# Nine places instead of seven in the ring of expert rows, the dot product written over its own input, and a 64 KB weight piece for the log gates

## The chip, the cores and the metric

The kernel runs on one core of a Trainium2 chip. The metric is the device time of one execution in microseconds (us). Below, PE is the matmul engine (PEld its weight load), DVE the vector engine, ACT the scalar engine, POOL the engine whose queue also issues the gathers, and SP the queue that issues the plain transfers.

## The reference

Two layers (`DEPTH = 2`) over 256 tokens of 1024 channels in float32. Each layer has a mixer and then an expert retrieval:

```
mix = _mixer(h, ...)                       # projections, gated linear attention, gMLP gating, output projection
h   = _layer_norm(ALPHA * h + mix, ...)
q   = (x @ wq)                             # 8 heads x 2 halves
v1, i1 = top_k(s1, 16); v2, i2 = top_k(s2, 16)
sc, pos = top_k(v1 + v2 of all pairs, 16)  # 16 experts per head: 128 per token
act = gelu(einsum('td,tkd->tk', x, u_tab[eidx]))
out = einsum('tk,tkd->td', softmax(sc) * act, v_tab[eidx])
h   = _layer_norm(ALPHA * h + out, ...)
```

Inside the mixer the log gates come from a narrow projection of 16 columns (`a @ w_gate_up + b_gate`, with `a` of rank 16).

## The kernel before, in words

The 256 tokens are two halves of 128 (one token per partition), so with two layers there are four blocks of retrieval, numbered 0 to 3: (layer 0, half 0), (0, 1), (1, 0), (1, 1). Each block has 128 steps, one for each of the 128 experts of a token, 512 steps in all. The tables `peer_u` and `peer_v` lie side by side in HBM, so a step fetches for each of the 128 tokens one row of 2048 floats, 8 KB.

One step `i` is made of these operations:

- `gather` (L726, POOL's queue): an indirect DMA of 128 rows of 8 KB into a tile `uv` of a ring of `UVBUFS = 7` places. It is issued `AHEAD - 1 = 4` steps early.
- `dot` (L733, DVE): multiplies the first 1024 columns of `uv` by the token's `h` and sums them into one column of `dots`. The elementwise product goes to a scratch tile `junk`.
- `weigh` (L739 to L742, ACT): gelu of the dot, times the softmax weight `ex`, spread on a diagonal matrix `dg` (three places).
- the product (L791, PE): `dg` times the last 1024 columns of `uv`, accumulated over the block in two PSUM banks `bank_acc`. Each product is recorded as four matmuls of 128x512. When it has run, the place in the ring is free.

Beside the 128 steps of a block runs the work of another block, as a generator `side(n, done)`: it finishes the block before (`residual_block`), computes the mixer of the next block (`front`) and its 128 expert numbers per token (`ask`, with the top-16 searches on DVE in `top16` and `retrieve`). After each step as many pieces of this generator are recorded as an allowance `PACE` lets through. A piece's cost is given by its `yield`. Side work of block 3 is only the output of block 2. PE, DVE and ACT execute in the order in which the code records the instructions (`manual_schedule`), while the framework places what POOL and SP do.

Layer norms need one instruction on POOL each, a power (`rrs`, `bnrs` or `ri`, at L161 and L215). It stands in the same queue as the gathers.

The mixer's and the query's weights come as pieces of 128x1024 floats, 512 KB, 45 for each of four passes (`feed_of`, `Feed`), through a ring `raw` of four. ACT rounds each piece to a high part `whi` (L142) and DVE forms the rest `wlo` (L147). The first piece of a pass is `C_A`, the 16 columns of the log gates, padded with zeros to 128 columns. The loop as it stands before:

```
if i > 1:
    m = i - 2
    ... nc.tensor.matmul(acc[hf], lhsT=dgs[m], rhs=uvs[m][...])
if i < N:
    dot(i // K % NB, i % K, uvs[i], chosen[i // K][2])
if 0 < i <= N:
    dgs[i - 1] = weigh((i - 1) % K, *chosen[(i - 1) // K][1:])
if i == 0 or (i > 2 and i % K == 1 and i < N):
    work, debt = side(i // K, acc), 0.0
```

Of the kernel before, what the change touches and what calls it, by code (L numbers as in the profile page):

```python
# [19 lines left out]
L = 2  # L20
T = 256
D = 1024
# [14 lines left out]
UVBUFS, AHEAD = 7, 5  # L37
# [8 lines left out]
C_Q, C_K, C_A, C_SV, C_V, C_R, C_SU, C_OUT, C_WQ = 0, 2, 4, 5, 9, 13, 17, 21, 29  # L46
NCH = 45


class Feed:  # L50
# [9 lines left out]
    def load(self):  # L60
        if self.srcs:
            self.raws.append(self.t.load(self.srcs.pop(0)))
# [37 lines left out]
class Trunk:  # L100
# [34 lines left out]
    def load(self, src):  # L135
        raw = self.raw()
        self.nc.sync.dma_start(raw, src)
        return raw

    def split_hi(self, raw):  # L140
        hi = self.ring.tile([128, 1024], F32R, name="whi", tag="whi", bufs=HI)
        self.nc.scalar.copy(hi, raw)  # L142
        return hi

    def split_lo(self, raw, hi):
        lo = self.ring.tile([128, 1024], F32R, name="wlo", tag="wlo", bufs=LO)
        self.nc.vector.tensor_tensor(lo, raw, hi.bitcast(F32), op=OP.subtract)  # L147
        return lo
# [45 lines left out]
    def wide(self, b, hi, lo, p=None):  # L194


        p = self.bank("a")[:, :256] if p is None else p
        v = p.rearrange("p (e t) -> p e t", e=2)
        for dc in range(DC):
            self.mm(v, [(hi[:, dc * 128:(dc + 1) * 128], self.x[:, b, dc])], dc == 0, False)  # L200
        for dc in range(DC):
            self.mm(v[:, 0], [(lo[:, dc * 128:(dc + 1) * 128], self.xh[:, b, dc])], False, dc == DC - 1)
        return v[:, 0], v[:, 1]
# [367 lines left out]
    def run(self):  # L571
        nc, a, sm = self.nc, self.a, self.sm
        with self.tc.tile_pool(name="peer", bufs=1) as pp:
# [193 lines left out]
            with self.tc.manual_schedule(engines=ORDERED):  # L767
# [13 lines left out]
                for i in range(N + 2):  # L781
# [4 lines left out]
                    if i > 1:  # L786
                        m = i - 2
                        if m % K == 0:
                            acc = [self.bank("acc") for _ in range(2)]
                        for hf in range(2):  # L790
                            nc.tensor.matmul(acc[hf], lhsT=dgs[m], rhs=uvs[m][:, D + hf * 512:D + (hf + 1) * 512],  # L791
                                             start=m % K == 0, stop=m % K == K - 1)
                        del dgs[m], uvs[m]
                    if i < N:
                        dot(i // K % NB, i % K, uvs[i], chosen[i // K][2])
                    if 0 < i <= N:
                        dgs[i - 1] = weigh((i - 1) % K, *chosen[(i - 1) // K][1:])
                    if i == 0 or (i > 2 and i % K == 1 and i < N):
                        for _ in work or []:
                            pass  # L800
                        work, debt = side(i // K, acc), 0.0
                    if work:
                        debt += PACE[min(i // K, 3)]
                        while debt > 0:
# [3 lines left out]
                            debt -= c or 1.5  # L808
                for _ in self.output_block(acc, 1, V_LN2 + V_LAYER):
# [30 lines left out]
def pack(inputs):  # L840
# [17 lines left out]
    wm[:, C_A].reshape(L, 128, DC, 128)[:, :, :, :16] = aw.reshape(L, DC, 128, 16).transpose(0, 2, 1, 3)  # L858
# [8 lines left out]
    for l in range(L):  # L867
# [5 lines left out]
        "vecs": vecs,  # L873
        "wmix": wm, "uv": uv,
# [23 lines left out]
```

## Time and profile before

| | |
|---|---|
| median of 3 runs | 1699.54 us (1698.48 to 1712.32) |
| profiled execution, its own time | 1692.46 us |
| span of the profiled execution | 1690.7 us |
| mean granted PE clock | 0.944 |
| bytes read from HBM | 634.38 MB |
| PE / DVE / ACT / POOL busy | 85% / 71% / 47% / 36% of the span |

The profiled execution is one of several, 1.8 us longer than its span and 7.1 us shorter than the median of the timed runs. The first 139 us have no gather; the last gather is issued at 1662 us. All times of the trace count from the start of the span. In a table of stretches, PEclk is the granted share of the full PE clock, and GB/s is what all DMA engines moved in the stretch.

### The profile page before, as it was taken

To read this page: it belongs to the slowest core of one execution; us is meant where nothing else is said; L and a number is where in the kernel's file an instruction comes from. 1 tells how busy PE (TensorE), PEld (TensorE's weight loads), DVE (VectorE), ACT (ScalarE), POOL (GpSimd) and SP (SyncE) were. 2 spreads that over 40 slices of the span, in tenths; PEclk is the share of its full clock that TensorE was granted. 3 is DMA by queue.
4 is the path that set the end of the run, shared out by engine and by line. 5 is a ranking of instruction groups with operands and counts; after the bars stand their busy time and mean duration, and the time that the engine had idled before them with its cause. 6 is when DMAs were issued, how large, how long until landed. Compare 5 with 4: busy or idle time off the path is not lost.

```text
span 1690.7 us, 17829 instructions
## 1 busy us (share of the span) xinstructions
PE 1430.4 (85%) x4544; PEld 749.1 (44%) x4544; DVE 1204.0 (71%) x2898; ACT 794.7 (47%) x2106; POOL 614.1 (36%) x542
## 2 busy tenths in 40 slices
PE   7887699989878889989887798989977887777776
PEld 5675255646533455445543354545543332222222
DVE  6778977767998667666898566766899654444444
ACT  5643465654544565544444374544444433333332
POOL 0002343444324343444334343444324433333331
PEclk9976999999899999999999898999989989999999
DMA  7647999999989999999989999999989999999996
GB/s 234 224 143 300 347 390 396 416 417 419 404 330 364 392 418 391 419 419 419 396 353 386 402 399 363 418 419 419 419 320 361 409 372 421 422 421 422 421 421 255
DMA packets 102409, 636.60 MB, mean 377 GB/s; under 512 B 11634, under 2 KB 12436, under 8 KB 36772
## 3 DMA queue, kind: packets, MB, share of 16 engines
q0 software_dynamic: 73872, 537.49, 78.3%
q1 hardware_dynamic: 28436, 97.98, 15.3%
q8 instruction: 37, 0.61, 0.1%
q14 instruction: 64, 0.52, 0.1%
HBM read 634.38 MB, written 1.05 MB: 376 GB/s over the span
## 4 chain that ended last, share of the span: by engine, by line
DVE 28%; DMA 24%; issue 19%; PE 14%; POOL 12%; ACT 2%; POOLq 1%; DVEq 0%; SPq 0%; ACTq 0%
DMA uv<-uv,eid 23%; POOL uv L726 11%; DVE junk L733 10%; PE bank_acc L791 7%; PE bank_a L153 5%; DVE wlo L147 3%; DVE i L605 2%; DVE v L603 2%; PE bank_b L179 1%; DVE S L608 1%; DVE sums L650 1%; POOLq L726 1%; DVE pos L605 1%; DVE sums L651 1%; ACT whi L142 1%
## 5 line engine op out<-in xcount | busy, mean ns | idle before, releaser
L791 PE MATMUL bank_acc<-uv,dg 128*128 128x512 f32 x2048 | 1012.3, 629 | 199.0 <-ACT dg L742 187.7
L726 POOL DMA_INDIRECT uv<-uv,eid x512 | 595.8, 1164 | 917.8 <-PE bank_acc L791 599.1
L733 DVE SCALAR_TENSOR_TENSOR junk<-uv,h 128x1024 f32<-128x1024 f32 x512 | 626.8, 1224 | 369.6 <-DMA uv<-uv,eid 364.6
L791 PEld LDWEIGHTS bank_acc<-uv,dg 128*128 128x128 f32 x2048 | 375.6, 196 | 723.4 <-ACT dg L742 383.9
L739 ACT ACTIVATE dots<-dots 128x1 f32<-128x1 f32 x512 | 103.3, 202 | 561.1 <-DVE junk L733 556.6
L147 DVE TENSOR_TENSOR wlo<-raw,whi 128x1024 fp32r<-128x1024 f32 x180 | 218.9, 1219 | 35.0 <-issue 16.9
L742 ACT ACTIVATE dg<-ident,dots 128x128 f32<-128x128 f32 x512 | 205.6, 402 | 38.5 <-PE bank_acc L791 21.9
L142 ACT CAST whi<-raw 128x1024 fp32r<-128x1024 f32 x180 | 187.4, 1044 | 42.9 <-DMA raw<-wmix 23.6
L740 ACT ACTIVATE dots<-dots,ex 128x1 f32<-128x1 f32 x512 | 150.8, 295 | 16.6
L153 PE MATMUL bank_a<-whi,x 128*128 128x512 f32 x384 | 137.2, 465 | 6.4 <-ACT f_sr L520 4.8
L153 PE MATMUL bank_a<-x,whi 128*128 128x256 f32 x672 | 118.9, 325 | 9.3 <-ACT f_half L694 6.1
L153 PEld LDWEIGHTS bank_a<-x,whi 128*128 128x128 f32 x672 | 98.2, 213 | 24.6 <-issue 9.8
L153 PEld LDWEIGHTS bank_a<-whi,x 128*128 128x128 f32 x384 | 72.7, 192 | 48.0 <-issue 27.4
L153 PE MATMUL bank_a<-x,wlo 128*128 128x128 f32 x672 | 91.1, 282 | 0.0
L153 PEld LDWEIGHTS bank_a<-x,wlo 128*128 128x128 f32 x672 | 89.5, 206 | 0.0
L179 PE MATMUL bank_b<-vecs,ident 16*128 16x512 f32 x96 | 58.9, 752 | 23.8 <-DVE f_at L408 11.9
L694 ACT COPY f_half<-bank_a 128x128 f32<-128x128 f32 x64 | 17.0, 265 | 113.6 <-DVE qp L697 109.1
L153 PE MATMUL bank_a<-wlo,x 128*128 128x512 f32 x192 | 66.6, 401 | 2.0 <-DVE wlo L147 1.9
L700 PEld LDWEIGHTS bank_b<-kt,qp 128*128 128x128 f32 x128 | 26.0, 214 | 40.6 <-issue 17.1
L179 PEld LDWEIGHTS bank_b<-vecs,ident 16*128 16x128 f32 x96 | 19.5, 219 | 55.2 <-issue 30.2
L153 PEld LDWEIGHTS bank_a<-wlo,x 128*128 128x128 f32 x192 | 36.3, 191 | 13.3 <-DVE wlo L147 5.2
L733 DVE DVE_READ_ACCUMULATOR junk<-uv,h 128x1 f32 x512 | 42.1, 82 | 0.0
(137 smaller groups left out, 761.6 us busy)
## 6 DMA issues: line engine op xcount, KB each, us to landing
raw<-wmix SPq DMA_DIRECT2D x180, 512.0 KB
uv<-uv,eid POOLq DMA_INDIRECT x512
h<-x SPq DMA_DIRECT2D x2, 512.0 KB
out<-h SPq DMA_DIRECT2D x4, 256.0 KB
f_cM<-gm POOLq DMA_DIRECT2D x1, 576.0 KB
f_sw<-sgwT SPq DMA_DIRECT2D x2, 256.0 KB
f_msk<-gmask SPq DMA_DIRECT2D x1, 320.0 KB
kt<-kT SPq DMA_DIRECT2D x2, 128.0 KB
```

Source lines behind the costliest of these rows:

```text
L142: self.nc.scalar.copy(hi, raw)
L147: self.nc.vector.tensor_tensor(lo, raw, hi.bitcast(F32), op=OP.subtract)
L153: self.nc.tensor.matmul(out, lhsT=l, rhs=r, start=start and i == 0, stop=stop and i == n - 1)
L179: self.nc.tensor.matmul(p, lhsT=self.ident[0:16, row:row + 1].to_broadcast([16, 128]), rhs=self.vecs[:, hf * 512:(hf + 1) * 512], start=Tr ...
L603: nc.vector.max(v[:, r], vals)
L605: nc.vector.max_index(i[:, r], v[:, r], vals)
L726: nc.gpsimd.indirect_dma_start(out=uv, out_offset=None, in_=a["uv"], in_offset=bass.IndirectOffsetOnAxis(ap=eid[:, k:k + 1], axis=0), boun ...
L733: nc.vector.scalar_tensor_tensor(junk, uv[:, :D], 1.0, self.h[:, b], op0=OP.mult, op1=OP.mult, accum_out=dots[:, k:k + 1])
L739: nc.scalar.activation(c, c, AF.Gelu)
L740: nc.scalar.mul(c, c, ex[:, k:k + 1])
L742: nc.scalar.mul(dg, self.ident, c)
L791: nc.tensor.matmul(acc[hf], lhsT=dgs[m], rhs=uvs[m][:, D + hf * 512:D + (hf + 1) * 512], start=m % K == 0, stop=m % K == K - 1)
```

## The change

`UVBUFS, AHEAD` become 9 and 8. The dot writes its elementwise product over the `u` half of its own place instead of `junk`. The product of step `m` is recorded at the end of step `m + 1`, after that step's side work, instead of at the head of step `m + 2`. The side work of a block starts at step 1, 129, 257, 385 (before: 0, 129, 257, 385). The `C_A` piece becomes an array of its own of 128x128 floats, 64 KB, and its matmuls write 16 rows instead of 128.

```diff
-UVBUFS, AHEAD = 7, 5
+UVBUFS, AHEAD = 9, 8
...
-C_Q, C_K, C_A, C_SV, C_V, C_R, C_SU, C_OUT, C_WQ = 0, 2, 4, 5, 9, 13, 17, 21, 29
-NCH = 45
+C_Q, C_K, C_SV, C_V, C_R, C_SU, C_OUT, C_WQ = 0, 2, 4, 8, 12, 16, 20, 28
+NCH = 44
+C_A = -1
...
-            self.raws.append(self.t.load(self.srcs.pop(0)))
+            src = self.srcs.pop(0)
+            raw = self.t.raw()[:, :src.shape[-1]]
+            self.t.nc.sync.dma_start(raw, src)
+            self.raws.append(raw)
...
+        m = hi.shape[-1] // DC
+        v = p[0:m].rearrange("p (e t) -> p e t", e=2)
         for dc in range(DC):
-            self.mm(v, [(hi[:, dc * 128:(dc + 1) * 128], self.x[:, b, dc])], dc == 0, False)
+            self.mm(v, [(hi[:, dc * m:(dc + 1) * m], self.x[:, b, dc])], dc == 0, False)
...
-                junk = pp.tile([128, D], F32, name="junk", tag="junk")
-                nc.vector.scalar_tensor_tensor(junk, uv[:, :D], 1.0, self.h[:, b], op0=OP.mult, op1=OP.mult,
+                u = uv[:, :D]
+                nc.vector.scalar_tensor_tensor(u, u, 1.0, self.h[:, b], op0=OP.mult, op1=OP.mult,
...
-                    if i > 1:
-                        m = i - 2
-                        if m % K == 0:
-                            acc = [self.bank("acc") for _ in range(2)]
-                        for hf in range(2):
...
-                    if 0 < i <= N:
+                    if i > 0:
                         dgs[i - 1] = weigh((i - 1) % K, *chosen[(i - 1) // K][1:])
-                    if i == 0 or (i > 2 and i % K == 1 and i < N):
+                    if i > 0 and (i - 1) % K == 0:
...
-                        work, debt = side(i // K, acc), 0.0
+                        work, debt = side((i - 1) // K, acc), 0.0
+                        acc = [self.bank("acc") for _ in range(2)]
...
+                    if i > 0:
+                        m = i - 1
+                        for hf in range(2):
+                            nc.tensor.matmul(acc[hf], lhsT=dgs[m], rhs=uvs[m][:, D + hf * 512:D + (hf + 1) * 512],
...
-        order += [C_WQ + k for k in range(16)]
-        return Feed(self, [self.a["wmix"][l, c] for c in order])
+        return Feed(self, [self.a["wa"][l] if c == C_A else self.a["wmix"][l, c] for c in order])
```

POOL's queue at the first gathers, before, with the semaphores that each instruction waits for (`DMASW0` to `DMASW7` tell of landings of POOL's DMAs, `PE` and `DVE` of those engines):

```order
L726 DMA uv<-uv,eid 128x2048 [waits DVE_49]
L726 DMA uv<-uv,eid 128x2048 x6
L726 DMA uv<-uv,eid 128x2048 [waits DMASW0_49,DMASW1_49,DVE_49,PE_49]
L726 DMA uv<-uv,eid 128x2048 [waits DMASW2_49,DVE_49,PE_49]
L726 DMA uv<-uv,eid 128x2048 [waits DMASW3_49,DVE_49,PE_49]
```

The same place after the change:

```order
L728 DMA uv<-uv,eid 128x2048 [waits DVE_49]
L728 DMA uv<-uv,eid 128x2048 x6
L728 DMA uv<-uv,eid 128x2048 [waits DMASW0_49]
L728 DMA uv<-uv,eid 128x2048 [waits DMASW1_49]
L728 DMA uv<-uv,eid 128x2048 [waits DMASW2_49,DVE_49,PE_49]
L728 DMA uv<-uv,eid 128x2048 [waits DMASW3_49,DVE_49,PE_49]
```

Nine gathers instead of seven stand ahead of the first that waits for PE. The landings are told by eight semaphores in turn, so from the ninth gather on each also waits for the landing of the one eight before it.

POOL's queue from the first gather of block 0 to the first powers, before:

```order
L726 DMA uv<-uv,eid 128x2048 x28
L215 TENSOR_TENSOR rrs<-rve,mhalf 128x1
L726 DMA uv<-uv,eid 128x2048 x17
L161 TENSOR_TENSOR bnrs<-rs,mhalf 128x1
L726 DMA uv<-uv,eid 128x2048 x21
```

And after:

```order
L728 DMA uv<-uv,eid 128x2048 x32
L217 TENSOR_TENSOR rrs<-rve,mhalf 128x1
L728 DMA uv<-uv,eid 128x2048 x17
L162 TENSOR_TENSOR bnrs<-rs,mhalf 128x1
L728 DMA uv<-uv,eid 128x2048 x21
```

Each power of block 0 stands behind four more gathers than before. In blocks 1 to 3 it is three more (at the first power of block 1: behind 138 gathers instead of 135).

PE in block 0, before, from a query of `ask` to the second row of products (L153 projects, L700 multiplies by the keys):

```order
L153 MATMUL bank_a<-x,whi 128x256 x8
L153 MATMUL bank_a<-x,wlo 128x128 x8
L700 MATMUL bank_b<-kt,qp 128x128
L153 MATMUL bank_a<-x,whi 128x256 x8
L153 MATMUL bank_a<-x,wlo 128x128 x8
L791 MATMUL bank_acc<-uv,dg 128x512 x4
L700 MATMUL bank_b<-kt,qp 128x128
```

And after:

```order
L154 MATMUL bank_a<-x,whi 128x256 x8
L154 MATMUL bank_a<-x,wlo 128x128 x8
L807 MATMUL bank_acc<-uv,dg 128x512 x2
L702 MATMUL bank_b<-kt,qp 128x128
L154 MATMUL bank_a<-x,whi 128x256 x8
L154 MATMUL bank_a<-x,wlo 128x128 x8
L807 MATMUL bank_acc<-uv,dg 128x512 x4
L702 MATMUL bank_b<-kt,qp 128x128
```

In block 0 the side work stands one product later (the program counts two matmuls to a product). From block 1 on, PE, DVE and ACT have the same order as before, side work and steps alike.

## Rows read from the trace of the kernel before

**Rows 1.** The page: engines, the gathers' queue, and the costliest groups.

```profile
PE 1430.4 (85%) x4544; PEld 749.1 (44%) x4544; DVE 1204.0 (71%) x2898; ACT 794.7 (47%) x2106; POOL 614.1 (36%) x542
...
q0 software_dynamic: 73872, 537.49, 78.3%
...
L791 PE MATMUL bank_acc<-uv,dg 128*128 128x512 f32 x2048 | 1012.3, 629 | 199.0 <-ACT dg L742 187.7
L726 POOL DMA_INDIRECT uv<-uv,eid x512 | 595.8, 1164 | 917.8 <-PE bank_acc L791 599.1
L733 DVE SCALAR_TENSOR_TENSOR junk<-uv,h 128x1024 f32<-128x1024 f32 x512 | 626.8, 1224 | 369.6 <-DMA uv<-uv,eid 364.6
```

**Rows 2.** Busy time by stretch: length; PE, PEld, DVE, ACT, POOL; PEclk, DMA share, GB/s.

```profile
139.00:240.00 101.00, 77.59 (x229) 39.74 (x228) 89.77 (x304) 45.72 (x122) 41.07 (x35) 0.86 0.95 365
240.00:440.00 200.00, 189.22 (x705) 112.26 (x704) 147.62 (x289) 113.72 (x281) 80.46 (x66) 0.97 1.01 413
440.00:540.00 100.00, 76.46 (x240) 38.66 (x239) 93.48 (x338) 45.37 (x126) 35.34 (x31) 0.91 0.91 352
540.00:580.00 40.00, 33.09 (x79) 13.80 (x78) 24.98 (x43) 16.66 (x48) 14.59 (x15) 0.91 0.98 395
580.00:820.00 240.00, 220.99 (x783) 124.84 (x783) 167.56 (x315) 130.51 (x334) 103.52 (x81) 0.97 1.01 413
820.00:920.00 100.00, 77.43 (x244) 39.98 (x244) 95.19 (x343) 45.14 (x126) 34.66 (x31) 0.91 0.94 369
920.00:980.00 60.00, 50.18 (x127) 21.80 (x126) 37.36 (x72) 25.12 (x75) 24.06 (x22) 0.91 0.96 391
980.00:1220.00 240.00, 219.76 (x774) 124.16 (x773) 165.68 (x316) 128.40 (x329) 98.56 (x80) 0.96 1.00 409
1220.00:1330.00 110.00, 84.93 (x264) 42.96 (x263) 102.74 (x358) 49.64 (x141) 42.03 (x37) 0.94 0.91 354
1330.00:1380.00 50.00, 43.16 (x79) 15.72 (x78) 26.80 (x47) 15.84 (x54) 19.57 (x19) 0.86 0.94 380
1380.00:1660.00 280.00, 222.70 (x450) 75.94 (x448) 138.14 (x224) 100.57 (x336) 111.78 (x114) 1.00 1.01 421
```

**Rows 3.** POOL's timeline at the end of block 0: start, length, in brackets the idle time before.

```profile
514.27 0.99 POOL L726 DMA_INDIRECT uv<-uv,eid  x1 [2.43 <-DVE S L608]
520.41 1.08 POOL L726 DMA_INDIRECT uv<-uv,eid  x1 [5.16 <-PE bank_acc L791]
...
555.37 0.99 POOL L726 DMA_INDIRECT uv<-uv,eid  x1 [1.49 <-PE bank_acc L791]
557.86 0.99 POOL L726 DMA_INDIRECT uv<-uv,eid  x1 [1.50 <-PE bank_acc L791]
```

**Rows 4.** POOL's timeline where block 2 passes into block 3.

```profile
1353.49 0.99 POOL L726 DMA_INDIRECT uv<-uv,eid  x1 [1.50 <-PE bank_acc L791]
...
1360.20 1.04 POOL L726 DMA_INDIRECT uv<-uv,eid  x1 [0.24 <-issue]
1370.16 1.33 POOL L726 DMA_INDIRECT uv<-uv,eid  x1 [8.93 <-PE bank_acc L791]
```

**Rows 5.** PE's timeline just behind that place.

```profile
1370.53 11.98 PE L791 MATMUL bank_acc<-uv,dg 128*128 128x512 f32 x27
```

**Rows 6.** The page: splitting the weight pieces, and their loads.

```profile
L147 DVE TENSOR_TENSOR wlo<-raw,whi 128x1024 fp32r<-128x1024 f32 x180 | 218.9, 1219 | 35.0 <-issue 16.9
...
raw<-wmix SPq DMA_DIRECT2D x180, 512.0 KB
```

**Rows 7.** POOL's timeline where block 1 passes into block 2.

```profile
961.23 0.56 POOL L215 TENSOR_TENSOR rrs<-rve,mhalf 128x1 f32<-128x1 f32 x1 [5.84 <-DVE rve L548]
962.21 1.04 POOL L726 DMA_INDIRECT uv<-uv,eid  x1 [0.42 <-PE bank_acc L791]
```

**Rows 8.** DVE's timeline at the same place.

```profile
965.68 1.40 DVE L232 SCALAR_TENSOR_TENSOR h<-h,rrs,bank_b 128x512 f32<-128x512 f32 x2
```

**Rows 9.** The gather's line alone by stretch: length, POOL busy, PEclk, DMA share, GB/s.

```profile
440.00:540.00 100.00, 35.34 (x31) 0.91 0.91 352
...
1400.00:1640.00 240.00, 94.91 (x97) 1.00 1.01 421
```

More of the change, by code (lines that the diff above doesn't have):

```diff
@@ L133, in raw @@
         return r
[L135 to L138, printed above, removed]
     def split_hi(self, raw):
         hi = self.ring.tile([128, 1024], F32R, name="whi", tag="whi", bufs=HI)
+        hi = hi[:, :raw.shape[-1]]
         self.nc.scalar.copy(hi, raw)
@@ L146, in split_lo @@
         lo = self.ring.tile([128, 1024], F32R, name="wlo", tag="wlo", bufs=LO)
+        lo = lo[:, :raw.shape[-1]]
         self.nc.vector.tensor_tensor(lo, raw, hi.bitcast(F32), op=OP.subtract)
@@ L197, in wide @@
         p = self.bank("a")[:, :256] if p is None else p
-        v = p.rearrange("p (e t) -> p e t", e=2)
+        m = hi.shape[-1] // DC
+        v = p[0:m].rearrange("p (e t) -> p e t", e=2)
         for dc in range(DC):
-            self.mm(v, [(hi[:, dc * 128:(dc + 1) * 128], self.x[:, b, dc])], dc == 0, False)
+            self.mm(v, [(hi[:, dc * m:(dc + 1) * m], self.x[:, b, dc])], dc == 0, False)
         for dc in range(DC):
-            self.mm(v[:, 0], [(lo[:, dc * 128:(dc + 1) * 128], self.xh[:, b, dc])], False, dc == DC - 1)
+            self.mm(v[:, 0], [(lo[:, dc * m:(dc + 1) * m], self.xh[:, b, dc])], False, dc == DC - 1)
         return v[:, 0], v[:, 1]
@@ L780, in run @@
                 work, debt, acc = None, 0.0, None
-                for i in range(N + 2):
+                for i in range(N + 1):
                     for j in range(0 if i == 0 else i + AHEAD - 1, min(i + AHEAD, N)):
@@ L785, in run @@
                         uvs[j] = gather(chosen[j // K][0], j % K)
-                    if i > 1:
-                        m = i - 2
-                        if m % K == 0:
-                            acc = [self.bank("acc") for _ in range(2)]
-                        for hf in range(2):
-                            nc.tensor.matmul(acc[hf], lhsT=dgs[m], rhs=uvs[m][:, D + hf * 512:D + (hf + 1) * 512],
-                                             start=m % K == 0, stop=m % K == K - 1)
-                        del dgs[m], uvs[m]
                     if i < N:
                         dot(i // K % NB, i % K, uvs[i], chosen[i // K][2])
-                    if 0 < i <= N:
+                    if i > 0:
                         dgs[i - 1] = weigh((i - 1) % K, *chosen[(i - 1) // K][1:])
-                    if i == 0 or (i > 2 and i % K == 1 and i < N):
+                    if i > 0 and (i - 1) % K == 0:
                         for _ in work or []:
                             pass
-                        work, debt = side(i // K, acc), 0.0
+                        work, debt = side((i - 1) // K, acc), 0.0
+                        acc = [self.bank("acc") for _ in range(2)]
                     if work:
-                        debt += PACE[min(i // K, 3)]
+                        debt += PACE[min((i - 1) // K, 3)]
                         while debt > 0:
@@ L808, in run @@
                             debt -= c or 1.5
+                    if i > 0:
+                        m = i - 1
+                        for hf in range(2):
+                            nc.tensor.matmul(acc[hf], lhsT=dgs[m], rhs=uvs[m][:, D + hf * 512:D + (hf + 1) * 512],
+                                             start=m % K == 0, stop=m % K == K - 1)
+                        del dgs[m], uvs[m]
                 for _ in self.output_block(acc, 1, V_LN2 + V_LAYER):
@@ L857, in pack @@
     wm[:, C_K:C_K + 2] = feat(k)
-    wm[:, C_A].reshape(L, 128, DC, 128)[:, :, :, :16] = aw.reshape(L, DC, 128, 16).transpose(0, 2, 1, 3)
     wm[:, C_SV:C_SV + 4] = tok(sv)
@@ L873, in pack @@
         "vecs": vecs,
+        "wa": cc(aw.reshape(L, DC, 128, 16).transpose(0, 2, 1, 3).reshape(L, 128, DC * 16)),
         "wmix": wm, "uv": uv,
```

## The prediction, made blind

> **What bounds the kernel now.** I read the page first: which engine is full, and who waits for whom [rows 1]. No engine is: PE is busy 85% of the span, DVE 71%. The two long waits point at each other. DVE stands 364.6 us in front of its dots until a gather has landed, and POOL stands 599.1 us in front of its gathers until a product on PE has freed a place. So the ring of `uv` turns in a circle of gather, dot, product and free place, and the question is in which stretches the DMA engines are the slow part of it, and in which the ring holds them up.
>
> The table by stretch answers that [rows 2]. In the last, where block 3 has no side work, the DMA engines move 421 GB/s and all else waits: gathers are issued 2.49 us apart (555.37 and 557.86 us, [rows 3]), the time that 1.05 MB (537.49 MB over 512, [rows 1]) takes at that rate. I take 421 as the full rate. Every other stretch falls short of it. Length times (1 - rate/421) is the time in which the DMA engines might have moved bytes and did not:
>
> - four stretches in which DVE is full: 139 to 240 (13.4 us lost), 440 to 540 (16.4), 820 to 920 (12.4), 1220 to 1330 (17.5). DVE is busy 89 to 95% there, with the top-16 searches between the dots.
> - three passages between blocks: 540 to 580 (2.5), 920 to 980 (4.3), 1330 to 1380 (4.9).
> - the middles: 240 to 440 (3.8), 580 to 820 (4.6), 980 to 1220 (6.8). PE is busy 92 to 95% there, and the rate is 409 to 413.
> - 1380 to 1660: nothing.
>
> That is 86.6 us in all, the most that feeding the DMA engines better could bring. How a loss looks is seen in two places. At the end of block 0, POOL issues a gather at 514.27 us and the next at 520.41 [rows 3]: all places hold landed rows, and the DMA engines stand until DVE and ACT have made the next `dg`. Between blocks 2 and 3, gathers go out at 1353.49, 1360.20 and then 1370.16 [rows 4], because PE is held up by the layer norm of the output. What is in flight runs dry before the last of them.
>
> **The ring.** Two more places let two more gathers go out before POOL has to wait. Two gathers are 2 x 2.49 = 5.0 us of DMA time. In a stretch where the ring fills, the DMA engines stop 5.0 us later, and when DVE comes free two more landed rows wait for it. The lead is kept only if the consumers can then go faster than the gathers. They can: behind the halt at 1370 PE runs 27 recorded matmuls, four to a product, in 11.98 us [rows 5], 1.77 us a product against 2.49 for a gather, and a dot takes 1.22 us [rows 1]. Each passage of the ring from empty to full and back thus gains the smaller of its loss and 5.0 us:
>
> - the four stretches with full DVE each lose more than 5.0: 4 x 5.0 = 19.9 us (exactly 4.98 each). The rest of their loss stays, since DVE has that much work.
> - the three passages lose less than 5.0 each, and close: 2.5 + 4.3 + 4.9 = 11.7 us.
> - the middles lose 15.2 us in many short waits. Each is covered by two places, but what PE may still give there is small: it is idle 10.8, 19.0 and 20.2 us, and part of that comes from the order of work, not from missing rows. Bounds 0 and 15.2; I take a third, 5.1 us, nearer to the lower end because of PE's 92 to 95%.
>
> **The product's new place.** From block 1 on nothing moves on PE, DVE and ACT: the product at the end of step m+1 and at the head of step m+2 has the same neighbours, and only POOL's gathers pass the side work's powers. In block 0 the side work comes one product and one dot later. DVE is full there from 139 to 240 and does the same work in another order: 0, with 1.3 us (a dot and its readout) either way.
>
> **Powers behind more gathers.** A power now stands behind three gathers more (four in block 0), the last of which waits for a product one step younger than before. At the passage into block 2 the power ran at 961.23, and the gather behind it followed the product that ended just before 962.21 [rows 7]. After the change that product, with a gather of 1.0 us, comes ahead of the power, so `rrs` is ready at about 963.9 instead of 961.8. Its reader on DVE starts at 965.68 [rows 8], so 1.8 us of cover remain. I price it at 0 and, at the thirteen powers, at up to 1 us each without cover, 13 us for the range.
>
> **The dot in its own place.** DVE's time goes by elements: the split `wlo`, two tensors into a third, takes 1219 ns, the dot 1224 [rows 1, 6]. Writing over an operand instead of `junk` changes neither count. I take 0. The row does not show a write into an operand, so I keep 0.1 us either way for each of the about 125 dots in the four full stretches, 12 us, for the range.
>
> **The small piece.** It saves 448 KB, 0.459 MB, in each of four passes [rows 6]. At 421 GB/s that is 1.09 us. Three of the passes are loaded beside gathers, in a kernel that would now be nearer to DMA's limit: 3.3 us. The first is loaded ahead of all gathers, where the DMA engines are not the limit: 0 to 1.1, I take 0. Its split gets some 1 us shorter on ACT and on DVE at each of the four places; at the passages this lies beside the residual that PE waits for, and the ring now covers that wait. I take 0, and up to 2 us.
>
> **Sum.** 19.9 + 11.7 + 5.1 + 3.3 = 40.0 us. The profiled execution took 1692.5 us, so it would take 1652.5. The median of the timed runs is 7.1 us above the profiled execution, which makes 1659.5 us, the forecast.
>
> **Rivals.**
>
> PE takes over. If PE's idle time in the middles is all structure, the leads won at 139 to 240 (5.0) and at the first two passages (6.8) find no spare PE time behind them and are lost, and the middles give nothing (5.1). That leaves 40.0 - 16.9 = 23.1 us: 1676.4. For it: windows in which PE is busy 92 to 95% [rows 2]. Against: these windows hold waits of DVE for rows too, which get shorter with the lead.
>
> POOL cannot issue. The gathers' issue could be what is short while DVE is full, not the places. Then the four stretches gain nothing, 40.0 - 19.9 = 20.1 us: 1679.4. In such a stretch 31 issues take 35.34 us, 1.14 each, against 0.98 (94.91 over 97) where DVE is half idle [rows 9]. That is 5 us of 100, and POOL stands idle most of the rest. The Trainium skill speaks for this rival (SBUF — State Buffer, "Summary: rules for kernel authors"): descriptors that GpSimd writes are starved while VectorE is in its faster modes. By that rule a deeper ring would be of no use exactly where DVE is full; the trace agrees with a longer issue, by 0.16 us, but not with starving.
>
> One place instead of two. The landings are counted by eight semaphores in turn, and the program's order shows a gather waiting for the landing of the one eight before it. If that binds, the ring acts as eight places: half of the 19.9 and about 2 us of the passages are lost, 28 us remain: 1671.5. Against it: a place is freed by a product, which needs the landing plus dot, weigh and product; so the landing of the younger neighbour, 2.49 us later, is mostly there already.
>
> The places are not the limit at all. Then the small piece alone counts, 3.3 us: 1696.2.
>
> Slower. The powers lock the circle: a power waits behind a gather, the gather for a product, the product on PE behind matmuls of side work that wait for the power before. If each of the thirteen cost two products and a gather on the path, 2 x 2.49 + 1.3 = 6.3 us, that is 82 us against 40: 1741. It decides from 40.0/13 = 3.1 us each. Against it are the 1.8 us of cover shown above, and that a place nine back was freed by a product from before the side work in question.
>
> **How the numbers follow.** Forecast 0.60 (gains of 30 to 50 us: 1650 to 1670). PE takes over 0.18, POOL 0.04, one place 0.06, no limit 0.05, slower 0.03, and 0.04 for more than 55 us, where the middles close wholly and PE's clock (0.86 to 0.97 in the stretches with waits) comes back. The range reaches from 1643, the sum with the middles' upper bound, the first piece and the shorter splits (53 us, with a few us for the spread of runs), to 1682, which takes in PE, POOL and one place and leaves out no limit, slower and some of the edges. A measurement of this kernel tells about 1%, 17 us, from no change. Faster by that much: 0.60 + 0.15 + 0.03 + 0.06 + 0.04 = 0.88. Within it: 0.09, mostly the no-limit case and the tails of PE and POOL. Slower: 0.03.
>
> **What the profile of the changed kernel would show.** The table by stretch: the four stretches with full DVE keep a dip, but each shorter by some 5 us of lost DMA time; the passages show 415 or more. The total wait of POOL for products falls by less than the wait of DVE for rows does, if PE becomes the limit in the middles. The dot's mean stays at 1.22 us and the gather's issue at about 1.0 to 1.2. POOL's first wait for a product comes behind nine gathers. The powers start 0 to 2.5 us later against their inputs, and their readers do not move. The bytes fall by 1.8 MB. The prediction is wrong if the middles come to run below 409 GB/s (PE, not DMA, sets them), if the full stretches lose as much as before (the issue or a semaphore limits), or if DVE waits for `rrs` at the passages.

## The result and the profile after

| | before | after |
|---|---|---|
| median of the timed runs | 1699.01 us (4 runs, 1696.97 to 1712.32) | 1649.27 us (4 runs, 1648.17 to 1650.77) |
| ratio after/before | | 0.9702, interval 0.9651 to 0.9752 |
| profiled execution, its own time | 1692.46 us | 1648.17 us |
| span | 1690.7 us | 1646.4 us |
| mean granted PE clock | 0.944 | 0.942 |

The change makes the kernel 3% faster. 1659.5 us was forecast; the miss is 10.2 us. The measured time is inside the range; the gain, 49.7 us, is at the upper edge of the 30 to 50 us to which the forecast itself gave a chance of 0.60.

The page of the changed kernel, with the lines that answer to [rows 1] and [rows 6], and the loads at its end (KB each, median us from issue to landing):

```profile
PE 1417.3 (86%) x4544; PEld 746.8 (45%) x4544; DVE 1191.3 (72%) x2898; ACT 790.2 (48%) x2106; POOL 636.8 (39%) x542
...
q0 software_dynamic: 73872, 537.49, 79.7%
...
L807 PE MATMUL bank_acc<-uv,dg 128*128 128x512 f32 x2048 | 1004.4, 627 | 174.1 <-ACT dg L744 166.7
L728 POOL DMA_INDIRECT uv<-uv,eid x512 | 620.1, 1211 | 887.4 <-PE bank_acc L807 572.7
L735 DVE SCALAR_TENSOR_TENSOR uv<-uv,h 128x1024 f32<-128x1024 f32 x512 | 618.6, 1223 | 313.0 <-DMA uv<-uv,eid 310.6
...
uv<-uv,eid POOLq DMA_INDIRECT x512, 17.3
...
raw<-wa SPq DMA_DIRECT2D x4, 64.0 KB, 6.7
```

DVE stands 310.6 us in front of its dots instead of 364.6, 54 us less, and the span is 44.3 us shorter. Work on the engines is almost the same. POOL's wait for products falls by only 26.4 us, from 599.1 to 572.7. The prediction had named this as what would be seen if PE became the limit in the middles, but the middles run faster than before (the table below), so this sign does not tell the two cases apart. The wait that moved with the span is that of DVE for rows.

The table by stretch, laid on the same places of the program as [rows 2] (length; PE, PEld, DVE, ACT, POOL busy; PEclk, DMA share, GB/s):

```profile
136.00:236.00 100.00, 73.84 (x214) 36.67 (x214) 86.16 (x302) 43.38 (x118) 43.69 (x37) 0.86 0.96 378
236.00:429.00 193.00, 186.43 (x704) 111.50 (x703) 145.57 (x266) 113.25 (x280) 82.81 (x66) 0.98 1.02 417
429.00:529.00 100.00, 75.50 (x253) 39.61 (x252) 95.37 (x366) 46.19 (x128) 35.73 (x31) 0.93 0.97 374
529.00:562.00 33.00, 31.37 (x88) 13.99 (x86) 23.43 (x43) 16.35 (x50) 17.28 (x16) 0.95 1.01 421
562.00:800.00 238.00, 219.47 (x774) 124.02 (x772) 166.74 (x311) 130.48 (x334) 105.11 (x81) 0.96 1.02 418
800.00:896.00 96.00, 76.33 (x243) 40.02 (x243) 91.78 (x344) 44.21 (x124) 34.94 (x31) 0.89 0.95 381
896.00:953.00 57.00, 51.72 (x136) 23.02 (x134) 38.62 (x75) 25.48 (x79) 29.38 (x24) 0.91 1.01 421
953.00:1186.00 233.00, 219.77 (x773) 124.87 (x772) 164.63 (x316) 127.97 (x328) 99.36 (x80) 0.96 1.01 416
1186.00:1290.00 104.00, 81.90 (x255) 41.56 (x254) 99.49 (x356) 48.50 (x138) 44.88 (x34) 0.93 0.94 376
1290.00:1336.00 46.00, 41.48 (x78) 15.95 (x77) 28.40 (x50) 15.94 (x55) 20.67 (x20) 0.85 1.01 421
1336.00:1615.00 279.00, 224.67 (x460) 78.22 (x458) 137.53 (x224) 100.55 (x338) 116.30 (x115) 1.00 1.01 421
```

The full rate is the same 421 GB/s. With length times (1 - rate/421), as in the prediction, the loss is 47.9 us where it was 86.6:

| stretch | lost before | lost after | gain | predicted |
|---|---|---|---|---|
| four with full DVE | 13.4, 16.4, 12.4, 17.5 | 10.2, 11.2, 9.1, 11.1 | 18.1 | 19.9 |
| three passages | 2.5, 4.3, 4.9 | 0, 0, 0 | 11.7 | 11.7 |
| three middles | 3.8, 4.6, 6.8 | 1.8, 1.7, 2.8 | 8.9 | 5.1 |
| small piece, three passes beside gathers | | | 3.3, as priced | 3.3 |
| start: first dot at 142.1 instead of 144.8 | | | 2.7 | 0 |

That is 44.7 us against the 44.3 by which the span fell. The small piece's 3.3 us are not read from a row; they are the saved bytes at the full rate. (The rates are rounded to 1 GB/s, some 0.2 us in 100.)

How a passage now looks is seen in POOL's timeline where block 2 passes into block 3, the place of [rows 4] (start, length, in brackets the idle time before and what ended it):

```profile
1313.60 0.99 POOL L728 DMA_INDIRECT uv<-uv,eid  x1 [1.51 <-PE bank_acc L807]
...
1319.57 0.99 POOL L728 DMA_INDIRECT uv<-uv,eid  x1 [4.99 <-DVE nm L252]
...
1330.42 1.13 POOL L728 DMA_INDIRECT uv<-uv,eid  x1 [9.25 <-PE bank_acc L807]
```

PE's halt is as long as before, 9.25 us without an issue on POOL against 8.93. But the DMA engines still have gathers in flight, and the stretch runs at 421 GB/s. Behind it PE catches up on the landed rows, as [rows 5] had promised:

```profile
1326.35 19.13 PE L807 MATMUL bank_acc<-uv,dg 128*128 128x512 f32 x39
```

Four matmuls to a product make this 1.96 us a product, against 2.49 for a gather.

The powers kept their cover. POOL and DVE where block 1 passes into block 2, as [rows 7, 8]:

```profile
935.39 0.99 POOL L728 DMA_INDIRECT uv<-uv,eid  x1 [5.31 <-PE bank_acc L807]
936.40 0.58 POOL L217 TENSOR_TENSOR rrs<-rve,mhalf 128x1 f32<-128x1 f32 x1
```

```profile
938.87 1.40 DVE L234 SCALAR_TENSOR_TENSOR h<-h,rrs,bank_b 128x512 f32<-128x512 f32 x2
```

`rrs` is ready at 936.98, its reader starts at 938.87: 1.9 us, where the prediction had worked out 1.8.

### The profile page after: what moved, and what is told of

It reads as the page before. It is cut to its first block, busy times and chain, and to the rows that moved or that the text cites. A ratio compares the mean times of both kernels' runs of the same rounds, so it can differ in the third digit from the quotient of the medians.

```text
span 1646.4 us, 17671 instructions
## 1 busy us (share of the span) xinstructions
PE 1417.3 (86%) x4544; PEld 746.8 (45%) x4544; DVE 1191.3 (72%) x2898; ACT 790.2 (48%) x2106; POOL 636.8 (39%) x542
## 4 chain that ended last, share of the span: by engine, by line
DVE 27%; DMA 26%; PE 23%; issue 17%; POOL 4%; ACT 2%; POOLq 0%; DVEq 0%; SPq 0%; ACTq 0%
DMA uv<-uv,eid 25%; PE bank_acc L807 13%; DVE uv L735 9%; PE bank_a L154 7%; POOL uv L728 4%; DVE wlo L148 3%; PE bank_b L180 2%; DVE i L607 2%; DVE v L605 2%; DVE S L610 1%; DVE sums L652 1%; ACT whi L142 1%; DMA raw<-wmix 1%; DVE sums L653 1%; DVE qp L699 1%
## 5 line engine op out<-in xcount | busy, mean ns | idle before, releaser
L728 POOL DMA_INDIRECT uv<-uv,eid x512 | 620.1, 1211 | 887.4 <-PE bank_acc L807 572.7
L735 DVE SCALAR_TENSOR_TENSOR uv<-uv,h 128x1024 f32<-128x1024 f32 x512 | 618.6, 1223 | 313.0 <-DMA uv<-uv,eid 310.6
L148 DVE TENSOR_TENSOR wlo<-raw,whi 128x1024 fp32r<-128x1024 f32 (+1 forms) x180 | 215.3, 1199 | 56.0 <-issue 20.5
L142 ACT CAST whi<-raw 128x1024 fp32r<-128x1024 f32 (+1 forms) x180 | 184.2, 1027 | 54.2 <-PE bank_a L154 29.6
L154 PE MATMUL bank_a<-x,whi 128*128 128x256 f32 (+1 forms) x672 | 119.0, 325 | 13.5 <-ACT f_half L696 10.6
L154 PEld LDWEIGHTS bank_a<-x,whi 128*128 128x128 f32 (+1 forms) x672 | 96.6, 208 | 29.9 <-ACT f_half L696 12.8
L154 PE MATMUL bank_a<-x,wlo 128*128 128x128 f32 (+1 forms) x672 | 88.5, 277 | 0.0
L154 PEld LDWEIGHTS bank_a<-x,wlo 128*128 128x128 f32 (+1 forms) x672 | 86.5, 199 | 0.3
L180 PE MATMUL bank_b<-vecs,ident 16*128 16x512 f32 x96 | 58.8, 749 | 19.2 <-DVE f_at L410 9.7
L735 DVE DVE_READ_ACCUMULATOR uv<-uv,h 128x1 f32 x512 | 42.5, 83 | 0.0
L192 ACT CAST x<-bank_b 128x512 fp32r<-128x512 f32 x24 | 13.7, 586 | 58.4 <-PE bank_b L189 58.3
## 6 DMA issues: line engine op xcount, KB each, us to landing
uv<-uv,eid POOLq DMA_INDIRECT x512, 17.3
```

The source lines that it names most:

```text
L154: self.nc.tensor.matmul(out, lhsT=l, rhs=r, start=start and i == 0, stop=stop and i == n - 1)
L180: self.nc.tensor.matmul(p, lhsT=self.ident[0:16, row:row + 1].to_broadcast([16, 128]), rhs=self.vecs[:, hf * 512:(hf + 1) * 512], start=Tr ...
L728: nc.gpsimd.indirect_dma_start(out=uv, out_offset=None, in_=a["uv"], in_offset=bass.IndirectOffsetOnAxis(ap=eid[:, k:k + 1], axis=0), boun ...
L735: nc.vector.scalar_tensor_tensor(u, u, 1.0, self.h[:, b], op0=OP.mult, op1=OP.mult, accum_out=dots[:, k:k + 1])
```

## The experiments

The theory after the result: the gain is the places' own. Each place keeps the DMA engines fed for 2.49 us more at every filling of the ring, until the stretch has no loss left. The order of the product, the dot over its own rows and the powers' new neighbours are worth nothing; the small piece is worth its bytes and what it gives at the start. Against it stood: that the new order makes part of the gain; that the eight landing semaphores stop the ring at eight places; that the small piece is worth more than its bytes; and that further places, paid for with other rings, give back what they bring. Each ratio is against the kernel before on the same chip in the same series.

**Seven, eight, ten places, and nine with the padded piece** (one series, the kernel before there 1700.22 us, 9 runs). The first two are the changed kernel with one line edited:

```diff
-UVBUFS, AHEAD = 9, 8
+UVBUFS, AHEAD = 7, 6
```

> The changed kernel with seven places again (gathers six ahead), everything else as changed: dot in its own place, product a step earlier in the record, small piece. Theory (the two places carry the gain: of the 86.6 us that the DMA engines lost before, 47.9 are left, so 38.7 us come from the places): 1649 + 39 = 1688 us, between 1683 and 1693, and the passages between blocks lose 10 to 12 us of DMA time again. Rival A (the new order of product, side work and gather carries it): 1665 us or less. Rival B (the small piece is worth much more than the 3.3 us priced): 1670 us or less.

```diff
-UVBUFS, AHEAD = 9, 8
+UVBUFS, AHEAD = 8, 7
```

> The changed kernel with eight places. Theory (a place is worth a gather, 2.49 us, at each stretch in which the ring fills, and the smaller of its loss and 2.49 us at a passage): the four full stretches lose 4 x 2.5 = 10 us more than with nine, the passages keep 2.5 each of their 11.7 and lose 4, the middles 2 to 4: about 1649 + 17 = 1666 us, between 1661 and 1671. Rival C (eight landing semaphores make nine places act as eight): the same as with nine, 1647 to 1652 us.

The tenth place needs room: the score tile `S` is put into the place of a mixer scratch tile that is dead by then.

```diff
-UVBUFS, AHEAD = 9, 8
+UVBUFS, AHEAD = 10, 9
...
-            m2 = tile_of("m2", [128, 2, 8, 128], tag="m2")
+            m2 = pp.tile([128, 2, 8, 128], F32, name="f_m2", tag="m2")
...
-                S = pp.tile([128, PH, 2, NK], F32, name="S", tag="S")
+                S = pp.tile([128, PH, 2, NK], F32, name="S", tag="m2")
```

> The changed kernel with ten places; the score tile S of the top-16 search shares its space with the mixer's tile m2 to make room, nothing else is changed. Theory: the four full stretches gain 4 x 2.5 = 10 us more, the passages nothing (they lose nothing with nine), the middles at most a few of their 6: about 1638 us, between 1635 and 1642. Rival C (the eighth landing back is the limit): 1647 to 1652 us. Rival D (sharing the tile makes the next block's mixer wait for the search): slower than 1650 us, with DVE or ACT waiting at the head of a block.

```diff
-C_Q, C_K, C_SV, C_V, C_R, C_SU, C_OUT, C_WQ = 0, 2, 4, 8, 12, 16, 20, 28
-NCH = 44
-C_A = -1
+C_Q, C_K, C_A, C_SV, C_V, C_R, C_SU, C_OUT, C_WQ = 0, 2, 4, 5, 9, 13, 17, 21, 29
+NCH = 45
...
-        return Feed(self, [self.a["wa"][l] if c == C_A else self.a["wmix"][l, c] for c in order])
+        return Feed(self, [self.a["wmix"][l, c] for c in order])
```

> The changed kernel with nine places, but the log gates' piece padded to 512 KB again. Theory: three passes beside gathers cost 1.09 us each, and the start before the first gather, which became 2.8 us shorter in the profile, goes back: 1649 + 3.3 + 2.8 = 1655 us, between 1652 and 1657. Rival E (the ring hides the pieces, and the start's 2.8 us are not the piece's): 1648 to 1651 us.

| kernel | median us (lowest to highest, runs) | ratio (interval) |
|---|---|---|
| ring7 | 1683.41 (1682.07 to 1686.61, 4) | 0.9909 (0.9884 to 0.9933) |
| ring8 | 1665.00 (1662.02 to 1666.44, 4) | 0.9789 (0.9765 to 0.9813) |
| nine places: the change itself, first measurement | 1649.27 (1648.17 to 1650.77, 4) | 0.9702 (0.9651 to 0.9752) |
| ring10 | 1634.83 (1633.20 to 1636.15, 5) | 0.9618 (0.9598 to 0.9637) |
| bigpiece | 1654.77 (1650.73 to 1659.67, 5) | 0.9748 (0.9725 to 0.9771) |

The ratio falls by 0.012, 0.009 and 0.008 per place, 18.4, 15.7 and 14.4 us between the medians: a falling return, as the theory has it. (Ring7, measured again below, comes out at 0.9948, which would make the first step 0.016.) A place gives up to 4 x 2.49 = 10 us in the four stretches with full DVE; the passages and middles bring the rest. Bigpiece gave the 1655 us that were expected, but its interval overlaps that of the change. Ring10 lies just below the 1635 to 1642 us of the theory; rivals C (1647 or more) and D (above 1650) fall. `AHEAD` moves with `UVBUFS` in every one of these edits, so a place and the earlier gather that fills it are tested together.

With seven places the passages are not closed. Three stretches of ring7 that answer to the passages, same columns as above:

```profile
534.00:574.00 40.00, 35.11 (x86) 14.83 (x85) 23.09 (x44) 16.23 (x50) 16.96 (x15) 0.87 0.96 389
...
914.00:974.00 60.00, 51.33 (x138) 21.29 (x136) 38.37 (x74) 26.89 (x82) 26.98 (x24) 0.97 1.01 410
...
1322.00:1371.00 49.00, 41.17 (x79) 15.58 (x80) 27.47 (x47) 16.19 (x55) 19.30 (x19) 0.90 0.98 398
```

They lose 3.0, 1.6 and 2.7 us; with nine places, nothing. That is 7.3 us together, where 10 to 12 had been expected.

The eight semaphores (rival C) do not stop the ring at eight, but they begin to show at ten. POOL's waits in front of the gathers (total us, times, longest), first of the changed kernel, then of ring10:

```profile
POOL uv L728 <- PE bank_acc L807: 572.7, 315, 14.5
```

```profile
POOL uv L728 <- PE bank_acc L807: 356.3, 182, 14.4
POOL uv L728 <- DMA uv<-uv,eid: 166.2, 139, 3.6
```

With ten places 139 gathers wait for a landing, that of the gather eight back. The page gives the median time from issue to landing:

```profile
uv<-uv,eid POOLq DMA_INDIRECT x512, 19.1
```

Eight gathers at 2.49 us are 19.9 us, so with ten places nearly eight are in flight at the median. The tenth place still brought 14.4 us by the medians. Some of that may be a landed row held for the time in which DVE comes free again; this is argued, not shown. What the trace shows is that the stretch that answers to 800 to 896 now loses 5.0 us instead of 9.1.

```profile
790.00:885.00 95.00, 73.75 (x249) 39.62 (x248) 90.95 (x349) 44.69 (x124) 36.44 (x29) 0.93 0.99 399
```

**The old order with nine places, the small piece alone, the new order with seven places, and eleven places** (another series; before 1694.37 us, 23 runs). Oldorder9 is the kernel before with two edits, so the product stays two steps behind, the side work starts at the old step, and the piece is padded:

```diff
-UVBUFS, AHEAD = 7, 5
+UVBUFS, AHEAD = 9, 7
...
-                junk = pp.tile([128, D], F32, name="junk", tag="junk")
-                nc.vector.scalar_tensor_tensor(junk, uv[:, :D], 1.0, self.h[:, b], op0=OP.mult, op1=OP.mult,
+                u = uv[:, :D]
+                nc.vector.scalar_tensor_tensor(u, u, 1.0, self.h[:, b], op0=OP.mult, op1=OP.mult,
```

> The kernel before with nine places (gathers six ahead) and the dot in its own place, but the old order of product, side work and gather and the padded piece. Against the nine-place kernel with the padded piece and the new order (1654.8 us). Theory (the order is worth nothing, since from block 1 on PE, DVE and ACT have the same one): 1655 us, between 1650 and 1660. Rival A (the order is worth some 11 us, which is what is left between the kernel before and seven places with all other edits, 16.8 us, once 5.5 us for the piece are taken off): 1663 to 1670 us.

Smallold is the kernel before with the array for the small piece, and nothing else of the change:

```diff
-NCH = 45
+NCH = 44
+C_A = -1
...
-        return Feed(self, [self.a["wmix"][l, c] for c in order])
+        return Feed(self, [self.a["wa"][l] if c == C_A else self.a["wmix"][l, c] for c in order])
```

> The kernel before with the small piece and nothing else. Theory: three passes of 1.09 us beside gathers and 2 to 3 us at the start, about 1694 us, between 1691 and 1697. Rival E (the piece is all of what seven places with the other edits gained, 16.8 us): 1683 us, between 1680 and 1687.

Ring7big is bigpiece with seven places:

```diff
-UVBUFS, AHEAD = 9, 8
+UVBUFS, AHEAD = 7, 6
```

> The changed kernel with seven places and the padded piece: the new order and the dot in its own place alone. Theory (both are worth nothing): 1700 us, between 1696 and 1704. Rival A (the order, or the dot's place, is worth about 11 us): 1689 us, between 1686 and 1693.

Ring11 is ring10 with another place, paid for with the rings of the weights:

```diff
-RAW, HI, LO = 4, 3, 2
-UVBUFS, AHEAD = 10, 9
+RAW, HI, LO = 3, 2, 2
+UVBUFS, AHEAD = 11, 10
```

> Ten places were 1634.8 us. This one has eleven, with S sharing the space of m2, and pays for the last place with one of the four places for raw weight pieces and one of the three for their high parts. Theory: the four full stretches gain 2.5 us each once more, about 1625 us, if the pieces still come in time. Rival F (the pieces come late: ACT and PE wait for raw or for a place for the high part): 1640 us or more, and the waits of ACT for raw or for PE's reading of the high part grow by more than 10 us. Rival C (no more than eight landings are told apart, so the eleventh place adds nothing): 1633 to 1637 us.

| kernel | median us (lowest to highest, runs) | ratio (interval) |
|---|---|---|
| oldorder9 | 1650.96 (1647.91 to 1652.31, 6) | 0.9730 (0.9704 to 0.9756) |
| smallold | 1692.10 (1686.22 to 1696.93, 12) | 0.9974 (0.9955 to 0.9992) |
| ring7big | 1699.28 (1690.67 to 1709.97, 12) | 1.0013 (0.9990 to 1.0036) |
| ring11 | 1657.26 (1653.57 to 1660.46, 6) | 0.9761 (0.9733 to 0.9788) |

Oldorder9 (0.9730) and bigpiece (0.9748) differ in the order alone and have the same ratio within their intervals, each on its own chip: no worth of the new order is seen with nine places (rival A, 1663 to 1670 us, falls). Ring7big says the same of seven, for order and dot together. The small piece alone gives 0.3%, some 2 to 4 us, not the 0.9% that ring7 had shown (rival E falls).

Ring11 is 1.4% behind ring10: the eleventh place was bought too dear, as rival F had it (1640 us or more, and ACT's waits grown by more than 10 us). ACT's waits in front of its rounding of the weights, ring10 and then ring11:

```profile
ACT whi L142 <- PE bank_a L154: 27.4, 16, 4.1
ACT whi L142 <- DMA raw<-wmix: 18.4, 12, 3.2
```

```profile
ACT whi L142 <- PE bank_a L154: 252.0, 119, 9.2
ACT whi L142 <- DMA raw<-wmix: 25.2, 11, 5.5
```

With two places for `whi` ACT stands 252 us until PE has used a piece. On ACT, in its fixed order, `weigh` stands behind that.

**The seven-place kernels once more, and the eleventh place paid otherwise** (a third series; before 1696.08 us, 21 runs). Ring7 had come out at the fast end of what was expected of it, and ring7big, which differs from it in the weight piece alone, 1.0% slower by the ratio. Ring7_again is ring7 unchanged:

> Seven places with all other edits, once more and on one chip with the next two. Alone, the piece gave 2.3 us and the new order with the dot in its own place nothing, each with seven places, but together they had given 16.8 us on another chip. Theory (the parts add up; the 16.8 us were the scatter of seven-place kernels, whose runs spread over 10 to 20 us): ratio to the kernel before 0.995 to 1.000, about 3 to 8 us faster. Rival G (the small piece and the new order help each other): ratio 0.989 to 0.993, 12 to 18 us faster.

Smallold_ip is smallold with the dot over its own rows (the last edit shown for oldorder9):

> The kernel before with the small piece and the dot in its own place, seven places, old order. Theory (the dot's place costs and gives nothing): the same as the small piece alone, ratio 0.995 to 0.999. Rival H (writing into the place instead of the scratch tile gives the 16.8 us together with the piece): ratio 0.989 to 0.993.

Ring7_junk is ring7 with the scratch tile back:

```diff
-                u = uv[:, :D]
-                nc.vector.scalar_tensor_tensor(u, u, 1.0, self.h[:, b], op0=OP.mult, op1=OP.mult,
+                junk = pp.tile([128, D], F32, name="junk", tag="junk")
+                nc.vector.scalar_tensor_tensor(junk, uv[:, :D], 1.0, self.h[:, b], op0=OP.mult, op1=OP.mult,
```

> Seven places, new order, small piece, but the dot's product into the scratch tile again. Theory: the same as seven places with all other edits, within 0.3%. Rival H (the dot's place matters): slower than that by 0.5% or more.

Ring11b keeps three places for `whi` and finds the rest in shared scratch tiles of the mixer (`lgh` and `lgl` in the place of `sr`, `ab` and `lg` in that of `vn`):

```diff
-RAW, HI, LO = 4, 3, 2
-UVBUFS, AHEAD = 10, 9
+RAW, HI, LO = 3, 3, 2
+UVBUFS, AHEAD = 11, 10
...
-        lgh = tile_of("lgh", [128, T], F32R)
-        lgl = tile_of("lgl", [128, T], F32R)
+        both_lg = tile_of("lgs", [128, 2, T], F32R, tag="f_sr")
+        lgh, lgl = both_lg[:, 0], both_lg[:, 1]
...
-            ab = tile_of("ab", [128, 256])
+            ablg = tile_of("ablg", [128, 512], tag="f_vn")
+            ab, lg = ablg[:, 0:256], ablg[:, 256:512]
...
-            lg = tile_of("lg", [128, 256])
```

> Eleven places, paid for with one of four places for raw pieces and with shared space (the log gates' scratch with vn and sr, S with m2), while the high parts keep their three places; the kernel with two of them lost 252 us of ACT's time to PE's reading. Theory (that wait was what ate the eleventh place): the four full stretches gain some 2.5 us each against ten places, so a ratio to the kernel before of 0.956 to 0.960 where ten places had 0.962. Rival C (eight landings in turn: an eleventh place adds nothing, since a gather also waits for the landing of the one eight back): 0.961 to 0.965. Rival F (three raw places are too few): 0.966 or more.

| kernel | median us (lowest to highest, runs) | ratio (interval) |
|---|---|---|
| ring7_again | 1687.14 (1680.23 to 1696.63, 12) | 0.9948 (0.9929 to 0.9968) |
| smallold_ip | 1686.14 (1680.43 to 1687.58, 6) | 0.9930 (0.9906 to 0.9954) |
| ring7_junk | 1687.33 (1680.01 to 1701.90, 10) | 0.9955 (0.9929 to 0.9981) |
| ring11b | 1640.40 (1638.63 to 1643.36, 5) | 0.9671 (0.9646 to 0.9695) |

Ring7_again lies between the two expectations: at 0.9948 it is just below the lower end of the one and above the upper end of the other. In the new order the scratch tile makes no difference, 0.9948 and 0.9955 (rival H falls there). Smallold_ip missed: the theory had 0.995 to 0.999, and 0.9930 is the upper end of what rival H had. Against smallold it would put 0.4% on the dot in the old order; the two ran on different chips, and their intervals (0.9906 to 0.9954, 0.9955 to 0.9992) almost touch, so this is inconclusive.

Ring11b lies behind ring10 by ratio, 0.9671 against 0.9618, on another chip: in the range of rival F (0.966 or more), not of the theory (0.956 to 0.960). The profiles, one of each, say where, against the kernel before: its first dot comes 3.8 us later, ring10's 5.5 earlier, 9.3 us lost at the start. There, in the first 133 us, ACT waits 15.3 us for raw pieces, in ring10 4.1. From the first dot to the last it gains 55.8 us, ring10 52.2. Over the whole span, ACT's wait for the raw pieces with three places for them is 95.3 us, against 18.4 in ring10:

```profile
ACT whi L142 <- DMA raw<-wmix: 95.3, 58, 5.7
```

So the eleventh place still brings 3.6 us in the gathers, and its price ahead of them is 9.3. **Ring10 is the best of all the kernels**: 3.8% faster than before, and by the ratios, taken in two series, 0.9% faster than the change.

**The ring apart from the start.** The profiles split the span further than the medians can: the start, the time from the first dot to the last, which is the ring's, and 15.5 us from the last dot on, the same in every profile. The dot's line (ns min/median/max, then the start of the first and of the last) in the kernel before, ring7, ring8, the change, bigpiece, oldorder9, ring10 and ring11b, in this order:

```profile
L733 DVE SCALAR_TENSOR_TENSOR junk<-uv,h x512: 1203/1225/1289, 144.8 to 1675.2; 128x1024 f32<-128x1024 f32 x171
L735 DVE SCALAR_TENSOR_TENSOR uv<-uv,h x512: 1204/1225/1296, 139.1 to 1665.2; 128x1024 f32<-128x1024 f32 x171
L735 DVE SCALAR_TENSOR_TENSOR uv<-uv,h x512: 1204/1225/1276, 138.5 to 1649.2; 128x1024 f32<-128x1024 f32 x171
L735 DVE SCALAR_TENSOR_TENSOR uv<-uv,h x512: 1204/1224/1295, 142.1 to 1630.9; 128x1024 f32<-128x1024 f32 x171
L734 DVE SCALAR_TENSOR_TENSOR uv<-uv,h x512: 1204/1224/1290, 142.8 to 1633.5; 128x1024 f32<-128x1024 f32 x171
L733 DVE SCALAR_TENSOR_TENSOR uv<-uv,h x512: 1204/1224/1301, 142.9 to 1630.7; 128x1024 f32<-128x1024 f32 x171
L735 DVE SCALAR_TENSOR_TENSOR uv<-uv,h x512: 1204/1224/1272, 139.3 to 1617.5; 128x1024 f32<-128x1024 f32 x171
L735 DVE SCALAR_TENSOR_TENSOR uv<-uv,h x512: 1203/1223/1272, 148.6 to 1623.2; 128x1024 f32<-128x1024 f32 x171
```

From the first dot to the last that is 1530.4 us before, then 1526.1 (seven places), 1510.7 (eight), 1488.8, 1490.7 and 1487.8 (nine), 1478.2 (ten) and 1474.6 (eleven). All seven profiles with seven places lie between 1526 and 1545, the three with nine between 1487 and 1491, whatever the order and the piece. Of the tenth place's gain 10.6 us stand here, about the 10 us of the four full stretches. The rest is mostly an earlier start (139.3 instead of 142.1), and the first dots in the eight profiles with the small piece and four raw places scatter from 138.5 to 142.1.

## Why the prediction was right, point by point

**What bounds the kernel.** Right: rows missing for DVE, because places came free too late. Of the 86.6 us of lost DMA time 38.7 came back, and the number of places moved the time in the same direction at each of the steps 7, 8, 9, 10.

**The full stretches.** 18.1 us against 19.9. One by one they gave 3.2, 5.2, 3.3 and 6.4 where 4.98 each was put. The sum holds within 10%; the single stretches do not. The rest stays lost, as said: DVE is 86 to 96% busy there.

**The passages.** 11.7 of 11.7: all three run at 421 GB/s, and the halt of PE stands there as before with work in flight.

**The middles.** The term that was most mis-sized in the stretches: 5.1 put, 8.9 measured, of a bound of 15.2. A third was taken because PE was busy 92 to 95%. The runs showed that PE had more to give: busy 92 to 97% of the middles after, at 416 to 418 GB/s. The first rival, PE takes over (1676.4 us), falls by the same rows.

**How sure this split is.** It rests on one profile of each kernel. Cut at the same dots of the program, the seven profiles with seven places lose 55.5 to 65.3 us in the full stretches, 5.4 to 21.5 in the passages and 15.5 to 22.8 in the middles; the three with nine lose 36.1 to 41.1, 0 to 1.0 and 5.7 to 6.2. So the 19.9 of the full stretches is borne out (19.2 between the middle values, 58.7 and 39.5), the middles gave some 9 to 17 instead of 5.1, and that the passages gave just 11.7 is luck: the kernel before is one draw from a wide scatter there.

**The small piece.** 3.3 us beside the gathers cannot be told apart in a profile. The start was put at 0 and gave 2.7 us between the two profiles; against bigpiece it gives 0.7 (142.8 to 142.1). That there is something is seen over all profiles: first dots at 138.5 to 142.1 us in the eight profiles with the small piece and four raw places, at 142.8 to 148.3 in the four with the padded one. By the medians the piece is worth 5.5 us with nine places (1654.77 against 1649.27, in two series), within the 3.3 to 6.4 that the prediction's bounds allowed, but the intervals of the two ratios overlap; alone it is worth 0.26%, about 4 us by the ratio and 2.3 by the medians.

**Product, powers, dot: 0 each.** Oldorder9 and bigpiece show no worth of the order with nine places. At the passage into block 2 the power keeps 1.9 us of cover. The dot's mean is 1223 ns instead of 1224, and ring7_junk shows no difference in time; in the old order the dot's place stays open (smallold_ip).

**POOL cannot issue.** The stretches that were to gain nothing by this rival gained 18.1 us with an issue as long as before. The gather's line alone, as [rows 9]:

```profile
429.00:529.00 100.00, 35.73 (x31) 0.93 0.97 374
...
1360.00:1600.00 240.00, 95.23 (x97) 1.00 1.01 421
```

That is 1.15 us an issue with full DVE against 0.98, as it was, while the rate of the stretch rose from 352 to 374 GB/s. The Trainium skill (SBUF — State Buffer, "Summary: rules for kernel authors") has the descriptors that GpSimd writes starved while VectorE is in its faster modes. The trace shows no starving, only an issue longer by 0.17 us. The prediction applied the rule to stretches where DVE is full, which is not what it says, and no run here shows in which mode DVE ran, so the rule itself is not tested.

**Where the 10.2 us are.** 4.3 are terms: the span fell by 44.3 us, not 40.0, the middles +3.8, the start +2.7, the full stretches -1.8 (the remainder is rounding). The other 6.0 are **the step from the profiled execution to the median**. It carried over 7.1 us, because the profile of before lay that far below the median; the profile of after lies 1.1 us below its own. The kernel before scatters (1687 to 1706 us over 23 runs of one series), and its one profile was at the low end; the changed kernel's runs lie within 2.6 us. The offset was one draw from a scatter, not a constant of the program.

**What stays open.** Why seven places scatter: ring7big, ring7_again and ring7_junk spread over 16 to 22 us, kernels with eight to ten, of 4 to 6 runs each, over 3 to 9. One sign is in the profiled run of ring7big, the slowest of its twelve. These two stretches at its last two passages

```profile
930.00:990.00 60.00, 50.43 (x109) 19.91 (x107) 34.33 (x65) 22.84 (x69) 23.32 (x22) 0.86 0.91 366
1340.00:1400.00 60.00, 50.36 (x93) 18.41 (x92) 30.26 (x54) 18.54 (x63) 24.12 (x23) 0.86 0.91 369
```

lose 15 us together, where ring7 loses 1.6 and 2.7 in its own. It is in the passages that the seven profiles with seven places differ most (5.4 to 21.5 us lost). Why is open: that a passage left open lets small differences in the order of events grow is argued, not shown. For the same reason the few tenths of a per cent between the seven-place kernels (small piece alone, with the new order, with the dot over its rows) are not settled. The 0.6% between ring7big (1.0013) and ring7_again (0.9948) was measured on two chips. Nor is the cause of the earlier start with the small piece shown, or its size, which is 0.7 us or 2.7 by the kernel that it is held against; that the pieces share the DMA engines with what the first matmuls wait for is argued.

## What to carry to other kernels

Before deepening a ring, cut the span into stretches, take the rate of the stretch in which the transfers run undisturbed, and write down length times (1 - rate/full rate) for each: a place more is worth its transfer time at each filling, up to the loss of that stretch. Here that gave 36.7 us for two places, and the rows show 38.7, with the middles mis-sized. Read the losses from more than one profile: those of a single one differ by several us in a stretch. Pay for places with dead scratch, not with another ring: what a third place for `whi` or a fourth for the raw pieces had hidden comes back as a wait, here on ACT in front of the weights. And do not carry the distance of one profiled execution from the median over to another kernel, when the kernel's runs scatter by more than the terms that are being summed.

## What the runs showed that I had not expected

A deeper ring went on paying when the number of transfers in flight came to its limit. From ten places on the gathers wait for the landing eight back (166.2 us in 139 waits), and the median time from issue to landing, 12.7, 15.2, 17.3 and 19.1 us for seven to ten places, comes near to eight gathers' 19.9; still the tenth place brought 10.6 us from the first dot to the last and the eleventh 3.6, by one profile of each. That they do so as landed rows in store for DVE is argued.

Scatter seems to go with the depth of the ring. The standard deviation of the runs is 2.1 to 7.1 us in the kernels with seven places and 1.1 to 3.8 in those with eight to eleven. The two groups overlap, and the deeper kernels have 4 to 6 runs each, so it is not settled.
